# Weight prefetch ahead of blocking waits, LayerNorm statistics by chunk, and tile entry woven into the output stage

## The chip, the cores and the metric

One Trainium2 chip, all eight NeuronCores, one program that runs once per call. The metric is device time in microseconds of the slowest core. Each core has TensorE (matmuls), VectorE, ScalarE, GpSimd, and a DMA queue fed by SyncE (SP). The granted clock is the share of TensorE's full speed that the profile records; the DMA share is the mean busy share of a core's 16 DMA engines. A transfer counts as landed at the time that the trace gives for its semaphore. Most executions agree within a fraction of a per cent. In some, one die (cores 0 to 3, or 4 to 7) runs at a lower granted clock and the time is some per cent longer. Such runs are called slow here and are left out of every comparison.

## The reference, cut to what matters

One layer of a hybrid decoder over a prompt (8 sequences of 2048 tokens plus 16 meta tokens) and a sample batch (128 sequences of 8 tokens). One prompt sequence goes to each core, and 16 sample sequences.

```python
def trunk_layer(x, h0_re, h0_im, conv_buf, p):
    proj = x @ p['w_in'] + p['b_in']            # [ssm u | conv GLU pair | gate_a | gate_b], 5 x 1024 columns
    ...
    y, h_re, h_im = s5_scan(u, h0_re, h0_im, ...)          # diagonal complex SSM
    z = jax.nn.gelu(y)
    za = z * jax.nn.sigmoid(z @ p['w_glu'] + p['b_glu'])
    pa = za @ p['w_a_out']
    glu = cg[..., :CONV_WIDTH] * jax.nn.sigmoid(cg[..., CONV_WIDTH:])
    cv = causal_depthwise_conv(hist, p['conv_w'], p['conv_b'])     # width 31
    cv = jax.nn.silu(layer_norm(cv, p['conv_ln_g'], p['conv_ln_b']))
    pb = cv @ p['w_b_out'] + p['b_b_out']
    mix = (gate_a * pa + gate_b * pb) @ p['w_o'] + p['b_o']
    x = layer_norm(ALPHA * x + mix, p['ln1_g'], p['ln1_b'])        # LN1
    hdn = jnp.square(jax.nn.relu(x @ p['w_ff1'] + p['b_ff1']))     # 1024 -> 4096
    ff = hdn @ p['w_ff2'] + p['b_ff2']
    x = layer_norm(ALPHA * x + ff, p['ln2_g'], p['ln2_b'])         # LN2
    return x, h_re, h_im, new_buf
```

An entry LayerNorm precedes the layer. Outputs are both `y`, the SSM states and the last 30 conv rows.

## The kernel before

Each core first converts its weights to bf16 in a prologue (to about 461 us). It then runs four prompt tiles of 512 tokens and a sample tile of 144 columns: 128 sample tokens and the last 16 tokens of the prompt. Activations lie with the features on the partitions. A tile goes: entry (load x, LayerNorm, transpose), in-projection of `u`, SSM input, GLU in two halves, conv, gates, output projections, LN1, feed-forward, LN2, output transposes, stores.

Weights stream in units of 1 MB through three slots of `WSL`. A unit is issued where it is used, so its issue stands in SP's program order behind whatever SP waits for there (in the first tile SP waits until 522.26, and the units of the first GLU half are issued from 522.69 on, core 5):

```python
class WStream:
    def load(self, spec, first_tile):
        sl = self.nxt
        self.nxt = (self.nxt + 1) % 3
        SP.wait(self.free[sl])
        ...
        ev = self.sem[sl].add(nc.sync.dma_start(out=dst, in_=src))
        return sl, ev
    def release(self, sl, ev):
        self.free[sl] = ev
```

The SSM stage shares one 4 MB buffer, `SSMW`, between two matrices. The second, `cssc`, may land only when the SSM input matmuls are done:

```python
        ssmw_free = e_mm                       # last SSM input matmul
        SP.wait(ssmw_free)
        ev_cs = ssmw_sem.add(nc.sync.dma_start(out=SSMW[:, :], in_=dr["cssc"]))
        ...                                    # the scan, on GpSimd
        for hh in range(2):                    # the two GLU halves
            slA, evA = WS.load(("mat", "in", 0, 2 + hh), first)
            slB, evB = WS.load(("mat", "in", 0, 4 + hh), first)
            PE.wait(evA, evB)
            ...                                # 64 matmuls
```

LayerNorm sums over partitions with a matmul against a matrix of ones. It waits for all eight chunks of the residual before the first cast, and for all casts before the first statistics matmul:

```python
        def ln_stats(src_bf, sq_bf, ready_evs):
            PE.wait(ready_evs)
            bM = BK.alloc()
            for kc in range(8):
                K.MM(PS[:, bM, 0:NT], lhsT=ONESB[:], rhs=src_bf[:, kc, 0:NT], ...)
            bQ = BK.alloc()
            for kc in range(8):
                last = K.MM(PS[:, bQ, 0:NT], lhsT=ONESB[:], rhs=sq_bf[:, kc, 0:NT], ...)
        def layer_norm_r32(ready, pre_free):
            ACT.wait(ready, pre_free)
            for kc in range(8):
                ACT.raw.activation(out=SBF[:, kc, 0:NT], in_=R32[:, kc, 0:NT], func=AF.Copy)
                evs.append(ACT.mark(ACT.raw.activation(out=SQ[...], in_=R32[...], func=AF.Square)))
```

The entry of a tile (load x, `bn_stats`, normalise on VectorE, eight transposes, evacuation on ScalarE and VectorE) starts when the tile before has issued all its output transposes.

Of the kernel before, what the change touches and what calls it, by code (L numbers as in the profile page):

```python
# [13 lines left out]
NCH = 8  # L14
# [560 lines left out]
def main_loop(K, ntiles=5, stop_after=None):  # L575
# [41 lines left out]

    class WStream:
        def __init__(self):
            self.nxt = 0  # L620
            self.free = [None, None, None]
            self.sem = [DmaSem(K, f"w{i}") for i in range(3)]

        def load(self, spec, first_tile):
            sl = self.nxt
            self.nxt = (self.nxt + 1) % 3
            SP.wait(self.free[sl])
# [22 lines left out]
            return sl, ev  # L650

        def release(self, sl, ev):
            self.free[sl] = ev

    WS = WStream()

    def wmat(sl):
        return WSL[:, sl, :].rearrange("p (kc n) -> p kc n", n=512)
# [17 lines left out]
    if dbg.get("only_last"):  # L676
        tiles = [tiles[-1]]

    chk("start", 0)
    for ti, T in enumerate(tiles):  # L680
# [26 lines left out]
        if isS:  # L707
            subt = [dict(c0=0, R=128, src=[(dr["xs"][0:128, :], 0, 128)], dst=[(dr["ys"][0:128, :], 0, 128)]),
                    dict(c0=128, R=16, src=[(dr["xp"][2032:2048, :], 0, 16)], dst=[(dr["yp"][2032:2048, :], 0, 16)])]
        else:  # L710
            subt = []
            for m in range(4):
                t0 = T["tok0"] + 128 * m
                if t0 == 0:
                    src = [(dr["meta"][0:16, :], 0, 16), (dr["xp"][0:112, :], 16, 128)]
                    dst = [(dr["yp"][0:112, :], 16, 128)]
                else:
                    src = [(dr["xp"][t0 - 16:t0 + 112, :], 0, 128)]
                    dst = [(dr["yp"][t0 - 16:t0 + 112, :], 0, 128)]
                subt.append(dict(c0=128 * m, R=128, src=src, dst=dst))  # L720

        if isS:
            SP.wait(ys_free[1])
            h0_sem.add(nc.sync.dma_start(out=H0S[:, :, 0, :], in_=dr["h0re"].rearrange("p (q s) -> p q s", s=NSEQ)))
            ev_h0 = h0_sem.add(nc.sync.dma_start(out=H0S[:, :, 1, :], in_=dr["h0im"].rearrange("p (q s) -> p q s", s=NSEQ)))
            POOL.wait(state.get("g16_free"))
            scf = dr["sconv_fm"].rearrange("p (k s r) -> p k s r", k=NCH, s=NSEQ)
            for k2 in range(4):
                ev_hist = hist_sem.add(nc.gpsimd.dma_start(out=GLUS[:, 2 * k2:2 * k2 + 2, :, 0:HP],
                                                           in_=scf[:, 2 * k2:2 * k2 + 2, :, :]))  # L730
            outs.add(nc.sync.dma_start(
                out=dr["ncv_s"].rearrange("(s r) d -> s r d", r=HP)[:, 0:HP - TC, :],
                in_=dr["sconv_nat"].rearrange("(s r) d -> s r d", r=HP)[:, TC:HP, :]))

        entry_evs = []
        for st in subt:
            c0, R = st["c0"], st["R"]
            sl = state["xs_i"] % 2
            state["xs_i"] += 1
            SP.wait(xs_free[sl])  # L740
            for (src, r0, r1) in st["src"]:
                ev_ld = xs_sem[sl].add(nc.sync.dma_start(out=XS[r0:r1, sl, :], in_=src))
            chk("e1", ti)
            DVE.wait(ev_ld)
            DVE.raw.bn_stats(ST6[0:R, sl, 0:6], XS[0:R, sl, 0:512])
            e = DVE.mark(DVE.raw.bn_stats(ST6[0:R, sl, 6:12], XS[0:R, sl, 512:1024]))
            DVE.wait(e)
            e = DVE.mark(DVE.raw.bn_aggr(MV[0:R, sl, :], ST6[0:R, sl, :]))
            DVE.wait(e)
            e = DVE.mark(DVE.raw.tensor_scalar(out=RS[0:R, sl, 0:1], in0=MV[0:R, sl, 1:2], scalar1=EPS,  # L750
                                               scalar2=None, op0=ALU.add))
            chk("e2", ti)
            POOL.wait(e)
            e = POOL.mark(POOL.raw.tensor_tensor(out=RS[0:R, sl, 1:2], in0=RS[0:R, sl, 0:1], in1=NHALF[0:R, :],  # L754
                                                 op=ALU.pow))
            DVE.wait(e)
            e_n = DVE.mark(DVE.raw.tensor_scalar(out=XS[0:R, sl, :], in0=XS[0:R, sl, :], scalar1=MV[0:R, sl, 0:1],  # L757
                                                 scalar2=RS[0:R, sl, 1:2], op0=ALU.subtract, op1=ALU.mult))
            chk("e3", ti)
            PE.wait(e_n, pev["ident"])  # L760
            for half in range(2):
                b = BK.alloc()
                for k4 in range(4):
                    kc = half * 4 + k4
                    ins = K.TR(PS[:, b, k4 * 128:k4 * 128 + R], XS[0:R, sl, kc * 128:(kc + 1) * 128],
                                              IDF[0:R, 0:R])
                e_t = PE.mark(ins)
                chk("e4", ti)
                if half == 1:
                    xs_free[sl] = e_t  # L770
                eng = ACT if half == 0 else DVE
                eng.wait(e_t, pev["derv"])
                for k4 in range(4):
                    kc = half * 4 + k4
                    src = PS[:, b, k4 * 128:k4 * 128 + R]
                    if eng is ACT:
                        ACT.raw.activation(out=XB[:, kc, c0:c0 + R], in_=src, func=AF.Identity,
                                           scale=V("ln_in_g", kc), bias=V("ln_in_b", kc))
                        ins = ACT.raw.activation(out=R32[:, kc, c0:c0 + R], in_=src, func=AF.Identity,
                                                 scale=DERV[:, 0, kc:kc + 1], bias=DERV[:, 1, kc:kc + 1])  # L780
                    else:
                        DVE.raw.tensor_scalar(out=XB[:, kc, c0:c0 + R], in0=src, scalar1=V("ln_in_g", kc),  # L782
                                              scalar2=V("ln_in_b", kc), op0=ALU.mult, op1=ALU.add)
                        ins = DVE.raw.tensor_scalar(out=R32[:, kc, c0:c0 + R], in0=src,  # L784
                                                    scalar1=DERV[:, 0, kc:kc + 1], scalar2=DERV[:, 1, kc:kc + 1],
                                                    op0=ALU.mult, op1=ALU.add)
                ee = eng.mark(ins)
                BK.release(b, ee)
                entry_evs.append(ee)
# [39 lines left out]
        SP.wait(ssmw_free)  # L829
        if first:  # L830
            SP.wait(pev["winsc"])
# [388 lines left out]
        for kc in range(8):  # L1220
# [6 lines left out]
            x1_evs.append(e)  # L1227

        chk("ln1", ti)
        s2_evs = {}  # L1230
        for hh in range(2):
            hd_evs = []

# [154 lines left out]
```

## Time and profile before

| | before |
|---|---|
| five runs, us | 2947.21 to 2989.55, median 2970.75 |
| profiled run: slowest core, span | core 5, 2946.1 us |
| from in-projection to in-projection, prompt tiles, us | 542.9, 542.4, 538.7, 538.6 |
| sample tile, in-projection to end, us | 293.0 |

The tile lengths are read from TensorE's timeline: the start of the first in-projection matmul of each tile. From the page of the kernel before, the busy line and the chain that ended last (shares of the span by engine; "DMA" there is time in which the last work waited for a transfer):

```profile
PE 1726.5 (59%) x14298; PEld 976.0 (33%) x14298; DVE 682.5 (23%) x1237; ACT 704.1 (24%) x1318; POOL 578.5 (20%) x1323
PE 55%; DVE 14%; DMA 10%; ACT 9%; another core or an unknown queue 7%; issue 4%; POOL 1%; SPq 1%; DVEq 0%; ACTq 0%; POOLq 0%
```

No engine is full. The last work hangs on TensorE for 55%, and for the rest on what TensorE waits for: 10% transfers, 14% and 9% chains of VectorE and ScalarE. Those three shares are what a change of order can reach.

### The profile page before, as it was taken

The page shows a single profiled execution, that of the slowest core. Times are in us where ns is not written, and L with a number is a line of the kernel's source. Part 1 is how long each engine was busy: PE and PEld are TensorE (multiplying, and loading weights), DVE is VectorE, ACT ScalarE, POOL GpSimd, SP SyncE. Part 2 cuts the span into 40 slices and gives each one's busy share as a digit, 9 for nine tenths or more (in the row PEclk, how much of TensorE's full clock was granted, in tenths as well). Part 3 has the DMA queues.
Part 4 walks back from the last instruction along what each step waited for, and adds up shares of the span by engine and source line. Part 5 has one row for each costly group of instructions (what it writes and reads, how often), then busy time and mean ns, then how long its engine had stood idle before and what let it go on. Part 6 is the DMA issues. An engine that isn't in the chain of part 4 may idle for free.

```text
span 2946.1 us, 37746 instructions; the slowest of 8 cores (2921.0 to 2946.1 us)
## 1 busy us (share of the span) xinstructions
PE 1726.5 (59%) x14298; PEld 976.0 (33%) x14298; DVE 682.5 (23%) x1237; ACT 704.1 (24%) x1318; POOL 578.5 (20%) x1323
## 2 busy tenths in 40 slices
PE   0010004589778269795945789596468976814645
PEld 0010002336333134462423336242333633314634
DVE  4850002111221500322032021402311122131121
ACT  0000093122232211314122131322212223221322
POOL 6000000640022037001201730031065002203001
PEclk9999999797889579877976896798669787956867
DMA  9999934442223334312414431241334222595445
GB/s 113 119 137 106 114 121 132 144 138 73 86 84 103 115 128 154 101 59 65 137 56 146 152 114 57 73 129 57 143 139 144 73 86 86 106 151 177 152 150 182
DMA packets 233776, 338.81 MB, mean 115 GB/s; under 512 B 29807, under 2 KB 213295, under 8 KB 231645
## 3 DMA queue, kind: packets, MB, share of 16 engines
q1 hardware_dynamic: 209261, 299.75, 31.8%
q0 software_dynamic: 24336, 36.64, 13.4%
q8 instruction: 117, 1.92, 0.3%
q14 instruction: 62, 0.51, 0.1%
HBM read 346.37 MB, written 63.73 MB: 139 GB/s over the span
## 4 chain that ended last, share of the span: by engine, by line
PE 55%; DVE 14%; DMA 10%; ACT 9%; another core or an unknown queue 7%; issue 4%; POOL 1%; SPq 1%; DVEq 0%; ACTq 0%; POOLq 0%
PE PS L112 53%; DMA WSL<-wsc_in 5%; ACT DG L539 2%; PE PS L116 2%; DVE TMPA L1022 1%; ACT B L1201 1%; ACT B L1202 1%; DMA WSL<-wsc_ff 1%; DVE TA L327 1%; ACT B L1222 1%; DVE R L1206 1%; DVE R L1209 1%; DVE R L784 1%; DVE B L782 1%
## 5 line engine op out<-in xcount | busy, mean ns | idle before, releaser
L112 PE MATMUL PS<-B,WSL 128*128 128x512 bf16 (+1 forms) x4160 | 840.4, 368 | 365.8 <-DMA WSL<-wsc_in 153.8
L112 PEld LDWEIGHTS PS<-B,WSL 128*128 128x128 bf16 x4160 | 400.2, 103 | 802.2 <-issue 444.0
L1241 POOL TENSOR_TENSOR G<-G 128x512 bf16<-128x512 bf16 (+1 forms) x160 | 146.5, 916 | 1176.6 <-ACT G L1237 1175.2
L112 PE MATMUL PS<-G,WSL 128*128 128x512 bf16 (+2 forms) x1528 | 272.4, 337 | 30.9 <-POOL G L1241 18.4
L112 PE MATMUL PS<-GLU,WSL 128*128 128x512 bf16 (+1 forms) x1240 | 240.8, 338 | 0.8 <-DMA WSL<-dsc 0.7
L116 PE MATMUL PS<-IDF,XS 128*128 128x128 f32 (+1 forms) x144 | 34.0, 415 | 286.8 <-DVE XS L757 286.8
L112 PEld LDWEIGHTS PS<-G,WSL 128*128 128x128 bf16 x1528 | 144.1, 101 | 158.5 <-issue 42.4
L1237 ACT ACTIVATE G<-PS,VECS 128x512 bf16<-128x512 f32 (+1 forms) x160 | 100.1, 626 | 307.4 <-PE PS L112 305.1
L1253 DVE TENSOR_TENSOR R<-PS,R 128x512 f32<-128x512 f32 (+1 forms) x80 | 49.2, 615 | 502.7 <-PE PS L112 502.5
L112 PE MATMUL PS<-B,KB 128*128 128x64 bf16 (+1 forms) x1440 | 150.4, 276 | 15.0 <-DVE HB L1086 12.7
L112 PEld LDWEIGHTS PS<-GLU,WSL 128*128 128x128 bf16 x1240 | 119.2, 97 | 119.6 <-issue 1.8
L112 PEld LDWEIGHTS PS<-B,KB 128*128 128x128 bf16 x1440 | 140.4, 122 | 20.0 <-issue 17.3
L116 PEld LDWEIGHTS PS<-IDF,XS 128*128 128x128 f32 (+1 forms) x144 | 27.6, 223 | 292.7 <-issue 292.7
L116 PE MATMUL PS<-IDB,WP 128*128 128x128 bf16 x128 | 14.9, 310 | 175.9 <-ACT WT L519 130.1
L112 PE MATMUL PS<-B,ONESB 128*128 128x512 bf16 (+1 forms) x240 | 63.8, 436 | 91.1 <-ACT B L1202 85.0
L1201 ACT ACTIVATE B<-R 128x512 bf16<-128x512 f32 (+1 forms) x80 | 44.2, 553 | 274.0 <-DVE R L1188 139.4
L881 POOL TENSOR_TENSOR SCR<-SCR,XH 128x64 f32<-128x64 f32 x274 | 95.7, 349 | 39.9 <-POOL SCR L880 0.9
L1017 DVE SCALAR_TENSOR_TENSOR TMPB<-PS,TMPA 128x512 f32<-128x512 f32 (+1 forms) x15 | 9.2, 615 | 398.6 <-ACT TMPA L1015 398.6
L882 POOL TENSOR_TENSOR XH<-SCR 128x64 f32<-128x64 f32 x274 | 88.7, 324 | 40.4 <-POOL SCR L881 1.7
L879 POOL TENSOR_TENSOR SCR<-XH,ARt 128x64 f32<-128x64 f32 x253 | 87.6, 346 | 37.4 <-POOL XH L882 1.7
L519 ACT ACTIVATE WT<-PS 128x1024 bf16<-128x1024 bf16 x16 | 15.3, 1026 | 325.1 <-DMA winsc<-WT 199.3
L754 POOL TENSOR_TENSOR RS<-RS,NHALF 128x1 f32<-128x1 f32 (+1 forms) x18 | 9.9, 548 | 402.2 <-DVE RS L750 402.2
(161 smaller groups left out, 1699.7 us busy)
## 6 DMA issues: line engine op xcount, KB each, us to landing
WSL<-wsc_ff SPq DMA_DIRECT2D x80, 1024.0 KB, 5.5
WSL<-wsc_in SPq DMA_DIRECT2D x50, 1024.0 KB, 8.0
WSL<-dsc SPq DMA_DIRECT2D x40, 992.0 KB, 6.0
SSMW<-winsc SPq DMA_DIRECT2D x5, 4096.0 KB, 20.6
SSMW<-cssc SPq DMA_DIRECT2D x5, 4096.0 KB, 15.4
wsc_ff<-w_ff POOLq DMA_DIRECT2D x4, 4096.0 KB, 297.5
wsc_in<-w_in POOLq DMA_DIRECT2D x5, 2048.0 KB, 65.7
WSL<-wsc_bout SPq DMA_DIRECT2D x10, 1024.0 KB, 6.4
```

The costliest lines, as they stand in the source:

```text
L112: return self.nc.tensor.matmul(*a, **kw)
L116: return self.nc.tensor.transpose(*a, **kw)
L327: return dv(DVE.raw.tensor_tensor(out=out, in0=a, in1=b, op=op))
L539: ins = ACT.raw.activation(out=DG[:, slot, jt, :], in_=IDB[:], func=AF.Identity, scale=VECS[:, col:col + 1])
L782: DVE.raw.tensor_scalar(out=XB[:, kc, c0:c0 + R], in0=src, scalar1=V("ln_in_g", kc), scalar2=V("ln_in_b", kc), op0=ALU.mult, op1=ALU.add)
L879: POOL.raw.tensor_tensor(out=m1, in0=hprev, in1=ARt[:], op=ALU.mult)
L881: pw(POOL.raw.tensor_tensor(out=t_, in0=m1, in1=xk_view, op=ALU.add))
L882: return pw(POOL.raw.tensor_tensor(out=xk_view, in0=t_, in1=m2[:, :, ::-1], op=ALU.add))
L1201: ACT.raw.activation(out=SBF[:, kc, 0:NT], in_=R32[:, kc, 0:NT], func=AF.Copy)
L1237: e = ACT.mark(ACT.raw.activation(out=HDN[:, ol, :], in_=PS[:, b, 0:NT], func=AF.Relu, bias=V("b_ff1", oc), scale=1.0))
L1241: e2 = POOL.mark(POOL.raw.tensor_tensor(out=HDN[:, ol, :], in0=HDN[:, ol, :], in1=HDN[:, ol, :], op=ALU.mult))
L1253: e = DVE.mark(DVE.raw.tensor_tensor(out=R32[:, oc, 0:NT], in0=PS[:, b, 0:NT], in1=R32[:, oc, 0:NT], op=ALU.add))
```

## The change

Its intent is to let TensorE wait less, with the same arithmetic and the same number of matmuls. The diff, cut to its core:

```diff
 class WStream:
-    def load(self, spec, first_tile):
-        sl = self.nxt
-        self.nxt = (self.nxt + 1) % 3
-        SP.wait(self.free[sl])
+    def pump(self, upto):                       # self.specs: all units of all tiles in order of use
+        while self.issued <= min(upto, len(self.specs) - 1):
+            j = self.issued
+            if j >= 3 and (j - 3) not in self.released:
+                break
+            self._issue(j)                      # slot j % 3
+            self.issued += 1
+    def load(self, spec, first_tile):
+        idx = self.taken
+        self.taken += 1
+        self.pump(idx + 2)
+    def release(self, j, ev):
+        self.released[j] = ev
+        self.pump(self.taken + 1)
 ...
         ssmw_free = e_mm
+        WS.pump(WS.taken + 2)                   # ahead of cssc's wait
         SP.wait(ssmw_free)                      # then cssc
 ...
         def ln_stats(src_bf, sq_bf, ready_evs):
-            PE.wait(ready_evs)
             bM = BK.alloc()
-            (8 matmuls of src_bf)
             bQ = BK.alloc()
             for kc in range(8):
+                PE.wait(ready_evs[kc])
+                (matmul of src_bf[kc])
                 (matmul of sq_bf[kc])
 ...
         def layer_norm_r32(ready, pre_free):
-            ACT.wait(ready, pre_free)
+            ACT.wait(pre_free)
             for kc in range(8):
+                ACT.wait(ready[kc])
 ...
+        if ti + 1 < len(tiles):                 # after the feed-forward, ahead of LN2
+            for q in subts[ti + 1][0:2]:
+                load_x(ti + 1, q)
 ...
         for st in subt:                         # output transposes and stores of one sub-tile
             ...
+            if ti + 1 < len(tiles):
+                (entry of the next tile's sub-tile whose columns are free now)
```

Moved besides: the load of `SSMW`'s first matrix goes into the LN1 of the tile before, the conv-state copy and the history loads of the sample tile go into the last prompt tile.

## The prediction

> **What bounds the kernel now.** I read the page first, then the waits of TensorE inside one prompt tile, then the timelines of TensorE and of the DMA-issuing queue around the largest waits, last the sample tile. The program is a prologue (to about 461 us on the profiled core), four prompt tiles of 512 tokens of about 542 us each, and a sample tile of 144 columns (from 2641.8 us). The waits of TensorE in the second prompt tile (us in total, times, longest):
>
> ```profile
> PE PS L116 <- DVE XS L757: 32.1, 4, 13.0
> PE PS L112 <- DMA WSL<-wsc_in: 28.7, 2, 23.4
> PE PS L112 <- ACT R L1225: 23.8, 1, 23.8
> PE PS L116 <- ACT R L1269: 21.1, 1, 21.1
> PE PS L112 <- ACT B L1202: 19.1, 2, 9.6
> PE PS L112 <- ACT B L1040: 11.5, 1, 11.5
> ```
>
> The second, fifth and much of the first row are what the change is aimed at; rows 3, 4 and 6 are LayerNorm chains that it leaves. TensorE is busy 388 us of such a tile, so the tile is bound by TensorE plus exposed waits, one after another. The same waits stand in every prompt tile: the first DMA one is 24.5, 23.4, 21.7 and 20.2 us long.
>
> TensorE's timeline of the first tile's end (start, length, work, idle before it and releaser):
>
> ```profile
> 776.61 13.97 PE L112 MATMUL PS<-B,WSL 128*128 128x512 bf16 x64 [1.74 <-DVE B L1174]
> 800.14 5.86 PE L112 MATMUL PS<-B,ONESB 128*128 128x512 bf16 x16 [9.56 <-ACT B L1202]
> ...
> 921.67 27.79 PE L112 MATMUL PS<-G,WSL 128*128 128x512 bf16 x128 [2.11 <-POOL G L1241]
> 959.04 4.93 PE L112 MATMUL PS<-B,ONESB 128*128 128x512 bf16 x16 [9.59 <-ACT B L1202]
> 985.06 5.62 PE L116 MATMUL PS<-IDF,R 128*128 128x128 f32 x32 [21.09 <-ACT R L1269]
> 1003.67 1.94 PE L116 MATMUL PS<-IDF,XS 128*128 128x128 f32 x8 [12.98 <-DVE XS L757]
> 1011.99 1.94 PE L116 MATMUL PS<-IDF,XS 128*128 128x128 f32 x8 [6.38 <-DVE XS L757]
> ```
>
> The reader sees that the 16 statistics matmuls (ONESB) start 9.6 us after the projection, though their inputs come one chunk at a time; and that from the output transposes (985.06) to the first matmul of the next tile (1033.46) 48.4 us pass. The DMA queue's own timeline shows the head of the line:
>
> ```profile
> 522.26 0.33 SPq L867 DMA_DIRECT2D SSMW<-cssc  x1
> 522.69 41.07 SPq L649 DMA_DIRECT2D WSL<-wsc_in  x4
> ...
> 624.99 25.73 SPq L649 DMA_DIRECT2D WSL<-wsc_in  x4
> ```
>
> The 4 MB cssc load waits until the SSM input matmuls end (522.2), and the weights of the GLU stage stand behind it in program order, though one slot was free before that. They land at 546.4.
>
> [...]a wait blocks every load issued after it; the trace agrees (522.26, then 522.69). [...]a load behind cssc also pays its transfer; the 22.8 us from issue to landing of these weights, against 5.5 for feed-forward weights, agrees. [...]16 statistics matmuls take 5.86 us after an idle wait and 3.61 us directly behind the convolution. [...]dense stretches read clock 1.00 and 217 ns per 512-column matmul, and all cores average 0.83.
>
> **The change, part by part.** The arithmetic and the number of matmuls stay.
>
> (1) Weights ahead of blocking waits. A list of units is pumped up to the three slots, at loads, at releases, and once ahead of cssc. Units 2, 3, 4 of a tile (both inputs of the first GLU half and one of the second) are then there before the SSM input stage ends. Gone: 24.5+23.4+21.7+20.2 = 89.8 us; I keep 0.4 each for handover: 88. The second GLU wait, 5.1 to 5.4 us per tile, stays: unit 5 needs the slot of unit 2, free only after the first half. The cssc transfer (15.4 us median) is about as long as that half (15.3 to 16.7), so it should not lengthen this wait by more than 1 us. The winsc load, moved into the previous LN1, was hidden before (0.9 us wait ahead of SSM input): 0.
>
> (2) LayerNorm statistics per chunk. The residual chunks come every 1.75 us (13.97/8), ScalarE's two casts take 1.04 us a chunk, and ScalarE is idle there, so it keeps pace. After the projection TensorE goes straight through 16 warm matmuls, 3.5 us; the last chunk (0.8 us evacuation, 1.15 us casts) is ready at 1.95. LN1: from 790.6 to 806.0 = 15.4 now, 3.5 then, saves 11.9. LN2: 949.5 to 964.0 = 14.5, saves 11.0. The chain after it (21 to 24 us) is unchanged. Four tiles: 91.6. The convolution's LayerNorm goes from 1.5+3.6 to 3.5, 1.6 each: 6.4; gate matmuls stall after 48 on banks held until that chain ends, so they profit from its earlier end.
>
> (3) Tile boundary. Entry of a sub-tile now follows its output transposes, with x already loaded. A sub-tile's serial chain is 8.32 us now (1003.67 to 1011.99), mostly in-order VectorE: statistics to normalised 3.7, transposes 1.2 to 2, evacuations 2.6. The new order adds VectorE's 0.69 output copy to each: 9.05. First statistics 2.75 us after the first output transpose, then 3x9.05 + 8.33 + 0.2 = 38.4 against 48.4: saves 10.0, three times, 30. The overlap is thus partial: the chain of VectorE stays. At the sample tile there are two entries: 2.75 + 9.05 + 6.7 = 18.5, plus about 2 for output transposes 3 and 4 in TensorE's order, 20.5 against 46.7 (2606.4 to 2653.1): 26. This includes the 1.4 MB conv-state copy and history loads that now go earlier.
>
> (4) Inside the sample tile (2653 to 2946), TensorE is small and loads count:
>
> ```profile
> 2674.87 0.33 SPq L867 DMA_DIRECT2D SSMW<-cssc  x1
> 2675.25 26.43 SPq L649 DMA_DIRECT2D WSL<-wsc_in  x4
> ...
> 2747.70 7.24 SPq L996 DMA_DIRECT2D ncv_s<-YS  x16
> 2754.99 0.42 SPq L998 DMA_DIRECT2D ncv_p<-XS  x1
> 2755.50 9.61 SPq L649 DMA_DIRECT2D WSL<-wsc_in  x4
> ```
>
> The first GLU half starts at once, but takes 6 us, so unit 5 now queues behind cssc. At the measured 6 MB in 20.4 us (3.4 us/MB), 5 MB land about 17.5 us after SSM input, the half takes 6.9: 24.4 against 39.2, saves 15 (not 20+6). Gates: 13.6 us wait behind the 17 state stores; two units now precede them, the others don't, and banks hold until the conv LayerNorm ends (2759.6): saves 7.5. The 9.0 us wait for glu weights behind the state-output stores goes: 9. Two narrow LayerNorms, ScalarE-bound: 3.5 each, 7. The 16 feed-forward loads, three slots deep, stay. Sum 38.
>
> Total 88 + 91.6 + 6.4 + 56 + 38 = 280 us. From the profiled 2947.2 this gives 2667.
>
> **The rivals.** (A) All waits named above vanish wholly, entry included. For it: the diff interleaves boundaries and prefetches everywhere. Then 18 more at each boundary and 12 in the sample tile: about 2590 to 2610. Against: VectorE's order is unchanged, and buffers number three as before. (B) DMA takes the place of the wait: cssc delays unit 5 by several us, winsc delays feed-forward weights, or SP, blocked in a prefetch wait, delays output stores. The 20 us GLU wait is partly replaced by a longer second one: 20 to 50 us back, about 2700 to 2720. For it: DMA share is 0.92 while cssc runs. Against: a prompt tile's mean DMA share is only 0.33. (C) [...]Dense stretches already run at 1.00 and TensorE busy per prompt tile only rises from 72% to about 80%; a 5% loss on 1500 us would be 75: about 2765. (D) The loads were hidden anyway: excluded by rows that show TensorE idle.
>
> **Range and chances.** The five times run from 2947.21 to 2989.55 with median 2970.75; the profiled one is the fastest, 23.5 below the median. I add that to 2667: 2690. Low end 2650: fast executions[...]. High end 2740: rival B in full plus some of C. Faster 0.98, same 0.015, slower 0.005: to stay within 2% (59 us) four fifths of measured idle would have to come back.
>
> **What would show it.** Right: SSM input followed within 1 us by GLU matmuls in prompt tiles, with the 5 us wait between halves kept; a statistics block starting within 0.5 us of its projection at about 3.5 to 4 us; first matmul of the next tile 37 to 40 us after the first output transpose, entry transposes about 9 us apart; prompt tiles near 485 us from in-projection to in-projection, sample tile near 255 from its in-projection to the end; TensorE busy about 1710. Wrong: a new wait of TensorE on WSL over 8 us in a prompt tile (B), dense stretches under clock 0.95 in fast runs (C), or boundaries under 30 us (A).

## The result, and the profile after

The changed kernel took 2685.86 us in the median of nine runs. Eight of them were fast, 2683.44 to 2691.6 us; the ninth was slow, 2910.67. (Three more executions of it are on record beside these: 2681.65, fast, and two slow ones of 2913.63 and 2916.24.) The ratio of the fast runs is 0.908, with a 95% interval of 0.9052 to 0.9108. All outputs are right. Ratios here are the mean time of one kernel's fast runs over that of the other's of the same rounds, so they are not quite the ratio of the medians.

The busy line and the chain that ended last, from the page of the changed kernel:

```profile
PE 1722.1 (64%) x14298; PEld 981.9 (37%) x14298; DVE 681.5 (25%) x1237; ACT 710.2 (26%) x1318; POOL 578.7 (22%) x1323
PE 60%; DVE 15%; ACT 7%; another core or an unknown queue 7%; DMA 5%; issue 5%; POOL 1%; DVEq 0%; SPq 0%; ACTq 0%; POOLq 0%
```

The numbers of instructions are the same, and the busy times agree within 1%. The share of transfers on the chain fell from 10% to 5%, that of ScalarE from 9% to 7%. VectorE's did not fall.

The ledger of tiles, slowest core of each profiled run (core 5 before, core 3 after):

| | before | predicted | after |
|---|---|---|---|
| prompt tiles, us | 542.9, 542.4, 538.7, 538.6 | near 485 | 489.3, 485.0, 484.4, 469.7 |
| sample tile | 293.0 | near 255 | 265.9 |
| span | 2946.1 | 2667 | 2684.7 |

The fourth length holds the short boundary to the sample tile. These are single cores: over the eight, the sample tile takes 286.1 to 293.0 us before and 257.3 to 267.7 after. The waits of TensorE in the second prompt tile after, to be held against the first view in the prediction (us in total, times, longest):

```profile
PE PS L112 <- ACT R L1282: 23.8, 1, 23.8
PE PS L116 <- ACT R L1341: 21.1, 1, 21.1
PE PS L116 <- DVE XS L765: 20.2, 4, 5.3
...
PE PS L112 <- DMA WSL<-wsc_in: 5.5, 1, 5.5
```

The two LayerNorm chains stand as they were. The statistics row (`ACT B`, 19.1) is gone, the weight row went from 28.7 to 5.5, the entry row from 32.1 to 20.2. The timeline of the first tile shows how the weights did it (start, length, work, idle before and its releaser). First the start of the first GLU half before, then the same stages after:

```profile
546.63 16.68 PE L112 MATMUL PS<-B,WSL 128*128 128x512 bf16 x64 [24.45 <-DMA WSL<-wsc_in]
```

```profile
507.85 14.96 PE L112 MATMUL PS<-B,SSMW 32*128 32x64 bf16 x512 [0.93 <-ACT B L876]
522.74 15.74 PE L112 MATMUL PS<-B,WSL 128*128 128x512 bf16 x64
548.06 16.71 PE L112 MATMUL PS<-B,WSL 128*128 128x512 bf16 x64 [9.58 <-DMA WSL<-wsc_in]
```

The first GLU half (522.74) follows the SSM input with no wait, where 24.45 us stood before. The second half still waits, because its last unit can be issued only when the first half frees a slot: that half ends at 538.48, the unit is issued at 538.57 and lands at 547.82. The end of the same tile:

```profile
917.19 3.62 PE L112 MATMUL PS<-B,ONESB 128*128 128x512 bf16 x16
941.90 1.94 PE L116 MATMUL PS<-IDF,R 128*128 128x128 f32 x8 [21.09 <-ACT R L1341]
948.16 1.94 PE L116 MATMUL PS<-IDF,XS 128*128 128x128 f32 x8 [4.32 <-DVE XS L765]
...
979.67 5.60 PE L112 MATMUL PS<-B,WSL 128*128 128x512 bf16 x16 [2.90 <-DVE R L793]
```

LN2's 16 statistics matmuls start without idle time and take 3.62 us at a granted clock of 1.00; before they took 4.93, at 0.73, after 9.59 us of idling. ScalarE's own timeline shows why: at LN1 of the same tile its casts began when the whole projection was done, and now there is a pair for each chunk, 1.73 us apart (before, then after):

```profile
791.47 0.63 ACT L1201 ACTIVATE B<-R 128x512 bf16<-128x512 f32 x1 [31.36 <-DVE R L1188]
792.00 0.61 ACT L1202 ACTIVATE B<-R 128x512 bf16<-128x512 f32 x1
792.52 0.61 ACT L1201 ACTIVATE B<-R 128x512 bf16<-128x512 f32 x1
```

```profile
759.76 0.63 ACT L1258 ACTIVATE B<-R 128x512 bf16<-128x512 f32 x1 [19.28 <-DVE R L1242]
760.30 0.61 ACT L1259 ACTIVATE B<-R 128x512 bf16<-128x512 f32 x1
761.49 0.63 ACT L1258 ACTIVATE B<-R 128x512 bf16<-128x512 f32 x1 [0.58 <-DVE R L1242]
```

From the first output transpose (941.90) to the next in-projection (979.67) 37.8 us pass, against 48.4.

The sample tile is where the ledger falls short. Cut at events that both timelines have, it reads:

| sample tile, from to | before | after | saved |
|---|---|---|---|
| in-projection to end of SSM input | 21.7 | 28.0 | -6.3 |
| to end of second GLU half | 39.2 | 26.3 | 12.9 |
| to end of conv statistics | 33.6 | 32.4 | 1.2 |
| to end of conv output projection | 31.8 | 27.8 | 4.0 |
| to start of the SSM's gate matmuls (`glu`) | 42.6 | 35.8 | 6.8 |
| to end of `o` | 19.8 | 21.4 | -1.6 |
| LN1 | 20.2 | 15.3 | 4.9 |
| feed-forward | 60.4 | 60.0 | 0.4 |
| to the end | 23.7 | 18.9 | 4.8 |

The first row is a loss that the prediction didn't have; in it the in-projection ran 1.5 us shorter and the SSM input stage 7.8 us longer. The same 512 small matmuls, before and then after:

```profile
2665.41 1.30 PE L112 MATMUL PS<-B,SSMW 32*128 32x18 bf16 x128 [3.27 <-issue]
2670.25 1.30 PE L112 MATMUL PS<-B,SSMW 32*128 32x18 bf16 x128 [3.54 <-issue]
2673.99 0.80 PE L112 MATMUL PS<-B,SSMW 32*128 32x18 bf16 x69 [2.44 <-issue]
```

```profile
2431.50 1.31 PE L112 MATMUL PS<-B,SSMW 32*128 32x18 bf16 x128 [5.04 <-issue]
2439.90 1.31 PE L112 MATMUL PS<-B,SSMW 32*128 32x18 bf16 x128 [7.10 <-issue]
2446.12 0.70 PE L112 MATMUL PS<-B,SSMW 32*128 32x18 bf16 x58 [4.90 <-issue]
```

"issue" means that TensorE waited for nothing that the profile shows. The stops come 128 matmuls apart, which with their 128 weight loads are 256 instructions. The three stops add up to 9.2 us before and 17.0 after. What else differs in these stretches is the DMA traffic (stretch, us, busy of each engine, granted clock, DMA share, GB/s), before and then after:

```profile
2660.31:2674.79 14.48, 5.23 (x512) 4.75 (x512) 0.52 (x2) 0.47 (x2) 0.00 (x0) 0.66 0.01 3
```

```profile
2424.53:2446.82 22.29, 5.24 (x512) 4.76 (x512) 0.52 (x2) 0.47 (x2) 0.00 (x0) 0.57 0.74 167
```

The traces list a DMA queue of the kind "instruction": in each of the two stretches it moved three packets, 0.05 MB together, and on the whole page it moved 117 packets of 1.92 MB, 16 KB each. The two `--dma` views of these stretches, before and then after, have it in one row each:

```profile
q8 instruction: 3, 0.05, 1.3%
```

```profile
q8 instruction: 3, 0.05, 1.2%
```

The DMA records of the traces show what ends the stops. In the kernel before the three packets start at 2663.1, 2667.9 and 2671.4, each in or at the edge of a stop. Over all eight cores of both kernels (48 stops) TensorE goes on 1.1 to 1.8 us after the end of an instruction packet, every time. A packet takes as long after as before (median 1.09 and 1.08 us); but it starts 2.4 us after the stop begins, where it started 0.1 us after it (medians). I read the stops, therefore, as waits for the next block of 256 instructions: the 128 matmuls of a block run in 1.3 us with 18 columns, and the next packet lands 1.1 to 1.8 us before TensorE goes on. Under the traffic of the changed kernel its transfer begins later.

SP's own timeline shows where the traffic of the changed kernel comes from:

```profile
2402.21 18.11 SPq L1369 DMA_DIRECT2D yp<-YS  x4
2423.31 0.66 SPq L842 DMA_DIRECT2D YS<-h0re  x1
2424.01 3.14 SPq L843 DMA_DIRECT2D YS<-h0im  x1
2427.26 7.22 SPq L668 DMA_DIRECT2D WSL<-wsc_in  x3
```

The interleaved entry stretches the output stores over 18.1 us (8.8 before), and the loads of the sample state and of three weight units, which stand behind them on SP, start at 2423 to 2434, inside the SSM input stage (2424.5 to 2446.8). The same stops, much smaller, came in the prompt tiles: with 64 columns, the second tile's SSM input has a stop of 1.3 to 2.8 us and the fourth's one of 1.8 to 2.6 us on every core, where the kernel before has at most 1.0 us at a time.

### The profile page after: what moved, and what is told of

It is laid out like the page before. It is cut to its first block, busy times and chain, and to the rows that moved or that the text cites. A ratio compares the mean times of both kernels' runs of the same rounds, so it can differ in the third digit from the quotient of the medians.

```text
span 2684.7 us, 37695 instructions; the slowest of 8 cores (2673.1 to 2684.7 us)
## 1 busy us (share of the span) xinstructions
PE 1722.1 (64%) x14298; PEld 981.9 (37%) x14298; DVE 681.5 (25%) x1237; ACT 710.2 (26%) x1318; POOL 578.7 (22%) x1323
## 3 DMA queue, kind: packets, MB, share of 16 engines
q8 instruction: 117, 1.92, 0.3%
## 4 chain that ended last, share of the span: by engine, by line
PE 60%; DVE 15%; ACT 7%; another core or an unknown queue 7%; DMA 5%; issue 5%; POOL 1%; DVEq 0%; SPq 0%; ACTq 0%; POOLq 0%
PE PS L112 57%; ACT DG L539 3%; PE PS L116 2%; DVE TMPA L1076 2%; DMA WSL<-wsc_in 1%; DVE TA L327 1%; DMA WSL<-wsc_ff 1%; ACT B L1279 1%; DVE R L1263 1%; DVE R L1266 1%; DVE B L791 1%; ACT R L1282 1%; DVE R L793 1%; DMA CIM<-cim 1%
## 5 line engine op out<-in xcount | busy, mean ns | idle before, releaser
L112 PEld LDWEIGHTS PS<-G,WSL 128*128 128x128 bf16 x1528 | 146.6, 103 | 157.8 <-issue 42.6
L112 PE MATMUL PS<-B,KB 128*128 128x64 bf16 (+1 forms) x1440 | 150.4, 276 | 15.4 <-DVE HB L1140 12.7
L112 PEld LDWEIGHTS PS<-B,KB 128*128 128x128 bf16 x1440 | 140.5, 122 | 20.3 <-issue 17.6
L519 ACT ACTIVATE WT<-PS 128x1024 bf16<-128x1024 bf16 x16 | 15.4, 1024 | 325.8 <-DMA winsc<-WT 199.9
L116 PE MATMUL PS<-IDF,R 128*128 128x128 f32 (+1 forms) x144 | 33.5, 416 | 95.0 <-ACT R L1341 95.0
L935 POOL TENSOR_TENSOR SCR<-XH,AI2t 128x64 f32<-128x64 f32 x253 | 87.7, 347 | 0.0
## 6 DMA issues: line engine op xcount, KB each, us to landing
SSMW<-winsc SPq DMA_DIRECT2D x5, 4096.0 KB, 20.5
```

Of the source, the lines that this page charges most:

```text
L112: return self.nc.tensor.matmul(*a, **kw)
L116: return self.nc.tensor.transpose(*a, **kw)
L935: pw(POOL.raw.tensor_tensor(out=m2, in0=hprev, in1=AI2t[:], op=ALU.mult))
```

## The experiments

My theory was that the terms of the prediction stand, each by its own mechanism; that the boundary which is left is VectorE's chain; and that the sample tile loses because data traffic makes its instruction blocks late (the fetch theory; an estimate of mine from the two stretches above, at DMA shares of 0.01 and 0.74, that no run settled). The rivals: that the gain comes from one part and the others ride along, that the boundary is bound by the load of x or by the order of the stages, and that the sample tile loses to its weights. On the second GLU wait I had two readings. The first, that cssc's transfer ahead of it lengthens it, is the one that I held at the start; the second, that it is only the time a unit takes to land once its slot is free. Each call ran on one chip with the kernel before beside it: experiments 1 to 4, 5 to 8, 9 to 12. "Saved" is the mean of the fast runs of the kernel before in that call (2939.7, 2950.7 and 2950.3 us) less that of the experiment.

| experiment | fast runs, us | ratio to before [95%] | saved |
|---|---|---|---|
| e1_ln_alone | 2835.49, 2834.16 | none (two fast runs) | 105 |
| e2_ln_undone | 2789.37, 2786.26, 2789.04 | 0.9485 [0.9464, 0.9506] | 151 |
| e3_no_lookahead | 2800.29, 2795.95, 2798.5 | 0.9519 [0.9498, 0.9541] | 141 |
| e4_entry_after_stores | 2682.49, 2678.9, 2685.97 | 0.9125 [0.9102, 0.9148] | 257 |
| e5_changed_again | 2705.81, 2683.77, 2683.67, 2689.35 | 0.9119 [0.9074, 0.9164] | 260 |
| e6_cssc_late | 2718.81, 2727.15 | 0.9229 [0.9198, 0.9259] | 228 |
| e7_early_stats | 2648.02, 2643.51, 2642.0, 2639.08 | 0.8953 [0.8935, 0.897] | 308 |
| e8_four_slots | 2627.99, 2658.67, 2627.85, 2631.37 | 0.8935 [0.8873, 0.8998] | 314 |
| e9_hold_in_sample | 2688.61 | one look | |
| e10_boundary_undone | 2715.64, 2738.25, 2717.34 | 0.9244 [0.9194, 0.9295] | 227 |
| e11_cssc_after_conv | 2682.78, 2681.22, 2686.91 | 0.9095 [0.9078, 0.9111] | 267 |
| e12_combined | 2572.64, 2571.99, 2568.92 | 0.8714 [0.8698, 0.8729] | 379 |

All gave right results.

**e1_ln_alone.** The kernel before, with the statistics part of the change alone (the same lines as in the diff above).

> The kernel before with only the LayerNorm part of the change (statistics matmuls and casts wait chunk by chunk). Theory (the parts add, each is worth what its wait showed): each of eight residual LayerNorms saves 11 to 12 us, each convolution LayerNorm 1.6, sample tile 7 in all: about 105 us, ratio to before 0.965. Rival (the parts overlap or the freed time returns in later waits, so one part alone gives much less): 50 us or less, ratio above 0.98.

105 us were saved, as expected. LN1's statistics start right behind the projection and take 3.62 us. So this part needs none of the others.

**e2_ln_undone.** The changed kernel with the statistics as before.

```diff
         def ln_stats(src_bf, sq_bf, ready_evs):
+            PE.wait(ready_evs)
             (8 matmuls of src_bf, then 8 of sq_bf)
-                PE.wait(ready_evs[kc])
         def layer_norm_r32(ready, pre_free):
-            ACT.wait(pre_free)
+            ACT.wait(ready, pre_free)
-                ACT.wait(ready[kc])
```

> The changed kernel with the LayerNorm statistics as before (one wait for all chunks, all sums, then all squares). Theory that the parts add: 105 us over the changed kernel, about 2790, ratio to before 0.943. Rival (loads prefetched early are hidden behind the longer LayerNorm, so part of the loss is refunded): 80 us or less. The wait of the statistics matmuls must be back at 9.6 us in every prompt tile in both readings.

It saves 151 us, 109 less than the changed kernel in its second measurement (e5). The wait for ScalarE's casts is back in the second tile, 19.1 us in two pieces, the very numbers of the kernel before:

```profile
PE PS L112 <- ACT B L1259: 19.1, 2, 9.6
```

Taken alone or taken away, the part is worth about the same.

**e3_no_lookahead.** The list of units stays, each is issued only where it is used.

```diff
-            self.pump(idx + 2)
+            self.pump(idx)
         def release(self, j, ev):
             self.released[j] = ev
-            self.pump(self.taken + 1)
-        WS.pump(WS.taken + 2)
```

> The changed kernel with each weight unit issued only where it is used, so behind the SSM output-weight load as before; everything else of the change stays. Theory: the first GLU wait returns at 20 to 24 us per prompt tile while the second falls to 5.1 to 5.4 from the 5.5 to 9.6 of the changed kernel, net about 80 us in four prompt tiles, and 15 to 25 us in the sample tile: about 100 us, 2785, ratio 0.942. Rival (weights were hidden anyway, the 108 us of LayerNorm and the boundary made the gain): below 30 us. In the sample tile the issue waits inside the SSM input stage fall from 17 us to about 9 if the prefetched weight loads cause the rest.

119 us less saved than in e5. In the first prompt tile TensorE again waits 33.9 us for these weights, 25.0 of them in one piece:

```profile
PE PS L112 <- DMA WSL<-wsc_in: 33.9, 2, 25.0
```

The 19 us above the expectation have a cause that I had left out: no unit is loaded during the boundary any more, so the sample tile's in-projection waits 16.2 us for its first. The stops in the sample tile's SSM input shrink (11.5 us on the profiled core, 9.4 in the median of the cores, DMA share 0.01), as the fetch theory wants.

**e4_entry_after_stores.** The entry follows all output sub-tiles, x is still loaded ahead.

```diff
             ys_free[sl] = ev_o
-            if ti + 1 < len(tiles):
-                done_cols = c0 + R
-                while nxt_i < len(subts[ti + 1]) and ... <= done_cols:
-                    emit_entry_sub(ti + 1, subts[ti + 1][nxt_i], e_t)
-                    nxt_i += 1
         if ti + 1 < len(tiles):
             while nxt_i < len(subts[ti + 1]):
```

> The changed kernel with the entries of the next tile emitted after all output sub-tiles, x still loaded early. My reckoning: the four output copies end 9.3 us after the first output transpose, then 4 times 8.32 us: 42.7 us from first output transpose to first matmul of the next tile instead of 37.8, so 4.9 us at each of three boundaries and about 5 at the sample tile: 20 us in all, ratio to before 0.915. Rival (interleaving is the worth of that part, early x only a detail): 10 us or more at each boundary, 40 us or more in all.

The profiled run was slow on one die; the other die's cores are read. The boundary is 42.0 us (core 3, from 926.84), 4.2 more than in the changed kernel and as expected. Yet the total is that of the changed kernel within the noise. The difference comes back in the sample tile, which is 249.5 to 253.4 us long to its last matmul on the four clean cores, against 253.8 to 264.2 on the eight cores of the changed kernel. SP's timeline on core 0 says why:

```profile
2403.15 5.52 SPq L1369 DMA_DIRECT2D yp<-YS  x4
2411.03 0.66 SPq L842 DMA_DIRECT2D YS<-h0re  x1
```

The stores are done in 5.5 us instead of 18.1, and the state and the weights come while TensorE still does the entry. On the clean cores the DMA share in the SSM input stage is 0.30 to 0.37, and the stops are 10.3 us in the median. So weaving entry and stores together gains 4 us at each of three prompt boundaries and 3.5 at the sample tile, some 16 us, and gives about 10 of them back inside the sample tile; the few us that should be left don't stand out of the noise.

**e5_changed_again.** The changed kernel beside the next three.

> The changed kernel itself, as the reference on the same chip as the next three, since the prologue ended 6 to 7 us earlier on the chip of the first four runs. 2675 to 2690, second GLU wait 5.5 to 10 us in prompt tiles, issue waits in the SSM input stage of the sample tile about 17 us.

It repeats: 0.9119 against 0.908, intervals overlapping. Differences below some 10 us between calls are therefore taken from tile lengths, not from ratios. One of its four fast runs, the profiled one of 2705.81, is an outlier (its first tile took 507 and 505 us on cores 0 and 1), and so is 2658.67 in e8. What is "saved beyond e5" below goes by the means of the table; by medians it is 44 us for e7 and 57 for e8.

**e6_cssc_late.** If cssc delays the second GLU wait's unit, moving cssc behind the GLU must shorten that wait.

```diff
         WS.pump(WS.taken + 2)
-        SP.wait(ssmw_free)
-        ev_cs = ssmw_sem.add(... cssc)
         ...
+        if not isS:                       # behind both GLU halves; in the sample tile behind the conv
+            SP.wait(ssmw_free)
+            ev_cs = ssmw_sem.add(... cssc)
         chk("glu", ti)
```

> The changed kernel with the SSM output-weight load moved behind the GLU stage (prompt tiles) or behind the convolution (sample tile). Theory (that load delays unit 5, the last GLU weights): the second GLU wait falls to 5.1 to 5.5 us in every prompt tile (8 us less in sum) and from 13 to about 5.5 in the sample tile; 10 to 15 us faster than the changed kernel in all. Rival (unit 5 is late only because its slot comes free late[...]): waits and time unchanged within 3 us.

Missed. It was 32 us slower than e5 (means of the fast runs; the profiled run was slow on one die, so a core of the other die is read). In prompt tiles the second wait didn't shrink (5.4 to 5.8 us in most, 8.3 in the first tile of core 5), and a new one appeared: cssc now stands ahead of the conv weights, and TensorE waits 9.8 us for them in that tile:

```profile
583.31 42.91 PE L112 MATMUL PS<-GLU,WSL 128*128 128x512 bf16 x186 [9.81 <-DMA WSL<-dsc]
```

In the sample tile the second wait did fall, to 5.4 to 8.1 us from 10.3 to 14.8. Moving a 4 MB load by one stage moved the collision by one stage.

**e7_early_stats.** Statistics and normalisation of the next tile's first two sub-tiles are done on VectorE during the second feed-forward half. If the boundary is VectorE's chain, it must shorten by what is taken out of it.

```diff
         for hh in range(2):
             hd_evs = []
+            if hh == 1 and ti + 1 < len(tiles):
+                for q in subts[ti + 1][0:2]:
+                    load_x(ti + 1, q)
+                for q in subts[ti + 1][0:2]:
+                    emit_entry_stats(ti + 1, q)      # bn_stats ... normalise, split off from the entry
 ...                                       (and load_x no longer ahead of LN2)
```

> The changed kernel with mean, variance and normalisation of the next tile's first two sub-tiles done during the second half of the feed-forward. Theory (in-order VectorE chain sets the boundary): first output transpose to next tile's first matmul falls from 37.8 to about 28 us at three boundaries, from 19.5 to about 12 at the sample tile; 35 us faster in all, about 1.3%. Rival (TensorE transposes or ScalarE's evacuations and the output stores bind there): 33 us or more at a boundary, under 15 us in all.

The boundary fell from 37.8 to 27.5 us and that to the sample tile from 19.5 to 8.8, 41 us over the four; 48 us were saved beyond e5. The first boundary on core 0:

```profile
939.43 1.94 PE L116 MATMUL PS<-IDF,R 128*128 128x128 f32 x8 [21.10 <-ACT R L1352]
941.16 1.91 PE L116 MATMUL PS<-IDF,XS 128*128 128x128 f32 x8
...
966.97 13.33 PE L112 MATMUL PS<-B,WSL 128*128 128x512 bf16 x52 [2.90 <-DVE R L802]
```

The entry's first transposes (`IDF,XS`) run with no wait. x was loaded ahead in both kernels, so it is VectorE's chain, and not the load, that bound the boundary.

**e8_four_slots.** A fourth weight slot, and a lookahead of one more. If the second GLU wait is a slot that comes free too late, it must go.

```diff
-    WSL = K.sb("WSL", [128, 3, 4096], BF16)
+    WSL = K.sb("WSL", [128, 4, 4096], BF16)
-            self.pump(idx + 2)
+            self.pump(idx + 3)
-            self.pump(self.taken + 1)
+            self.pump(self.taken + 2)
 ...                                       (slot numbers modulo 4, and the other two pumps, alike)
```

> The changed kernel with four weight slots and one unit more lookahead. Theory (the second GLU wait is a slot wait, made longer by the load ahead of it): it vanishes in prompt tiles, 29 us in sum; in the sample tile the 13 us wait goes too[...], so 10 to 20 us there: 40 to 50 us faster. Rival (the DMA engines bind there): the wait moves to the convolution's weights and the gain is under 20 us.

Gone, in every prompt tile: both halves are one block. On core 0, the first tile:

```profile
525.29 29.82 PE L112 MATMUL PS<-B,WSL 128*128 128x512 bf16 x128
```

54 us were saved beyond e5: 9.8, 7.0, 10.2 and 10.1 in the prompt tiles and 20.3 in the sample tile (slowest core against core 3 of e5, the sample tile to its last matmul). The prompt tiles gain more than their waits there (9.7, 5.4, 7.0 and 6.8 us). The clock was lower with the wait, too: in the changed kernel's first tile the second half's 64 matmuls read a granted clock of 0.83 and took 16.7 us, and both halves together 32.45; here all 128 take 29.8 at 0.93. In the sample tile the wait moved on in part: TensorE waits 9.55 us for the first conv weights, which now stand behind cssc.

**e9_hold_in_sample.** Meant as the direct test of the fetch theory: no weight prefetch while the sample tile's SSM input runs.

```diff
-            self.pump(idx + 2)
+            self.pump(idx if self.hold else idx + 2)     # the same at releases; hold: in-projection and SSM input of the sample tile
```

> The changed kernel, but in the sample tile no weight unit is loaded ahead until its SSM input matmuls are done. Theory[...]: the three issue waits of the SSM input stage fall from 14 to 17 us in sum to 9 to 12 (9.2 in the kernel before), and the first GLU half then waits 5 to 9 us for its weights, so the total hardly moves. Rival (the issue waits come with the tighter order[...]): still 14 us or more.

Void. The edit moved the loads in program order, but nothing between the old place and the new one makes SP wait, so they were issued at the same time (2427.7 against 2427.3) and the stops were the same 17.1 us. Here a later line alone didn't hold a load back. A wait on a semaphore did: in the kernel before, SP waits for the SSM input matmuls, which end at 522.2, and issues cssc at 522.26.

**e10_boundary_undone.** Entry after the stores, and x loaded only then.

```diff
-        if ti + 1 < len(tiles):
-            for q in subts[ti + 1][0:2]:
-                load_x(ti + 1, q)
 ...
-            (the entry of the next tile between the output sub-tiles, as in e4)
-            (the early load of x for the third and fourth sub-tile)
```

> The changed kernel with the boundary as before: entries after all output stores, x loaded only then. From first output transpose to next tile's first matmul 48 us again at three prompt boundaries (10.5 more than the changed kernel), about 38 to 45 instead of 19.5 at the sample tile; less the 10 us that the sample tile gained in the run with the entries after the stores. About 40 to 50 us over the changed kernel, near 2730, ratio 0.926. Rival (later stages absorb it): under 25 us.

The boundary is 47.8 us, within 0.6 of the kernel before. With e4 this splits the 10 us: 5.8 from the early load of x, 4.2 from the interleaving. The boundary to the sample tile is 29.1 us and not the 38 to 45 that I expected, for most of its gain isn't undone here. In the kernel before, x stood on SP's queue behind the state loads and the conv-state copy, and was issued 22.2 us after the first output transpose (2606.38); here it stands ahead of them, 9.2 us after (2423.31). Before, then here:

```profile
2624.74 3.81 SPq L731 DMA_DIRECT2D ncv_s<-sconv_nat  x1
2628.60 0.56 SPq L742 DMA_DIRECT2D XS<-xs  x1
```

```profile
2432.52 0.42 SPq L743 DMA_DIRECT2D XS<-xs  x1
```

In all 34 us less saved than in e5, below the 40 to 50 expected for that reason and because the sample tile's SSM input got its 4 us back.

**e11_cssc_after_conv.** As e6, but cssc goes behind the conv stage, so no weight unit of GLU or conv stands behind it.

```diff
-        SP.wait(ssmw_free)
-        ev_cs = ssmw_sem.add(... cssc)
 ...
         chk("conv", ti)
+        SP.wait(ssmw_free)
+        ev_cs = ssmw_sem.add(... cssc)
```

> The changed kernel with the SSM output-weight load moved behind the convolution in all tiles, where TensorE later waits 11 us for the conv LayerNorm anyway. Theory (the load costs whatever weight load stands behind it, and here there is slack): second GLU wait 5.1 to 5.5 us, no new wait on the convolution's weights, 5 to 12 us faster than the changed kernel. Rival (there is no free place for 4 MB in the tile): again slower, as when it stood behind the GLU stage.

As fast as the changed kernel within the noise, not 5 to 12 us faster. Over 32 prompt tiles (eight cores) the second GLU wait has a median of 5.66 us, 5.77 in the changed kernel and 5.40 in the kernel before. So in prompt tiles cssc isn't the cause, and that rival is out: the wait is the time that a 1 MB unit takes to land after its slot came free (a median of 5.6 us from issue to landing for the 50 units of `wsc_in` in the changed kernel). In the sample tile cssc was part of the cause: there the second-half wait fell to 5.5 to 7.0 us, from 10.3 to 14.8. Yet the tile is hardly shorter (256.3 to 260.3 us to its last matmul over the cores, against 253.8 to 264.2).

**e12_combined.** Four slots, cssc behind the conv, statistics of the first three sub-tiles early (three x slots, paid for by placing a small staging buffer in one of them), and the sample state loaded behind the SSM input. (In program order only: as in e9, nothing makes SP wait there, and the trace has the state loads inside that stage.)

> All that helped: four weight slots, the SSM output-weight load behind the convolution, statistics and normalisation of the next tile's first three sub-tiles during the feed-forward, state loads of the sample tile behind its SSM input stage. If gains add (44 for the early statistics, 57 for the slots, some 16 for the third sub-tile, 5 to 10 for the load): 120 us under the changed kernel, 2560 to 2575. If they overlap in the sample tile: 2580 to 2600. Ratio to before 0.87 to 0.88.

2571.2 us in the mean of the fast runs, ratio 0.8714: some 4% below the changed kernel (0.8714 / 0.9119 = 0.956). The gains of e7 and e8 add up (48 + 54 beyond e5 would be 362 saved; 379 were). On core 2 of the undisturbed die the prompt tiles take 460.0, 460.4, 460.9 and 444.2 us. The largest waits left in a prompt tile are the two LayerNorm chains, 23.8 and 21.1 us.

**What the three undoings add up to.** e2, e3 and e10 cost 109, 119 and 34 us, together 261 before rounding, the whole gain. I don't read this as proof that the parts are independent: e3 pays 16 us in the sample tile that the kernel before didn't, and the conv-state copy and the history loads, which were moved, are undone in none of the three.

**The fetch theory over runs.** The sample tile's SSM input stage, medians over the eight cores (of e4, e6 and e12 over the four of the undisturbed die), from the timelines of runs that were made for other reasons:

| kernel | DMA share in the stage | stops, us | stage, us |
|---|---|---|---|
| before | 0.02 | 8.1 | 13.3 |
| e3_no_lookahead | 0.01 to 0.02 | 9.4 | 14.6 |
| e4_entry_after_stores | 0.30 to 0.37 | 10.3 | 15.5 |
| e10_boundary_undone | 0.28 to 0.36 | 10.8 | 16.1 |
| e7_early_stats | 0.53 to 0.93 | 11.4 | 16.6 |
| e6_cssc_late | 0.85 to 0.90 | 12.9 | 18.2 |
| e8_four_slots | 0.77 to 0.93 | 14.3 | 19.6 |
| changed | 0.72 to 0.89 | 15.4 | 20.6 |
| e12_combined | 0.79 to 0.88 | 16.2 | 21.6 |

The stops are long where the traffic is dense, though the order isn't strict (e3 has next to none and longer stops than the kernel before; e6 is as dense as the changed kernel). That the stops end with the landing of an instruction block is shown above. That data traffic is what makes the block late stays unproven, since e9 failed. Nor is it the weights alone: in e4 and e10 the stage holds 1.3 to 1.9 MB of weights but not the state loads, whose short packets (under 512 B) are 8272 of the changed kernel's 11347 there (slowest core), and their stops are among the short ones. No run tells the two kinds of load apart.

## Why the prediction was right, point by point

The total was right: 2690 predicted, 2685.86 measured. Two errors in it nearly cancelled. The saving was put at 280 us and is 261.4 (2946.1 less 2684.7), 18.6 too much. And 23.5 us were added because the kernel before's median lay that far above its profiled run; the changed kernel's fast runs lie within some 8 us of each other, so this add-on should have been near zero. That the total came within 5 us is luck; what holds is the four terms below, one by one.

- **Weights ahead of blocking waits (88).** The first GLU wait went wholly in all prompt tiles, 89.8 us. The second was to stay at 5.1 to 5.4 and not grow by over 1 us. It stayed; its median over all cores grew by 0.4 us, but on the profiled core it was 9.58, 5.46, 6.96 and 6.66, 7 us more than before in sum. Net about 83.
- **Statistics (91.6 + 6.4).** LN1 was to fall from 15.4 to 3.5 and is 3.45; the conv's block was to take 3.5 and takes 3.6. In sum the twelve blocks of the prompt tiles end 99.6 us sooner after the work before them. e1 and e2 put the whole part, sample tile included, at 105 and 109, where its terms sum to 91.6 + 6.4 + 7 = 105.
- **Boundary (30 + 26).** 38.4 predicted, 37.8 to 38.0 measured at the three; 20.5 predicted at the sample tile, 19.5 measured; 58 us in all. (The prediction's 9.05 for 8.32 + 0.69 should be 9.01, which changes nothing.) The entries' transposes were to come about 9 us apart and come 8.8 to 8.9 apart. e7 confirms the reason given, VectorE's chain: with part of it done earlier the boundary fell from 37.8 to 27.5 us.
- **Sample tile (38).** This is the term that was mis-sized: 27.1 measured. Of its pieces the GLU (15 predicted, 12.9), the gates (7.5; 1.2 + 4.0) and the `glu` weights (9; 6.8) fell 6.6 us short together, and the two LayerNorms (7; 4.9 and part of 4.8) were met. What the sum lacked altogether is the stretch up to the end of the SSM input, 6.3 us longer. The prediction had counted the loads that move there as free, because TensorE needed no weights from them; yet the packets of TensorE's instructions came later there (2.4 us after a stop began, against 0.1, in the median). I had the stops in front of me in the profile before (9.2 us) and passed over them as a constant.
- **Rivals.** A (all waits vanish, 2590 to 2610) is out: entry and second half wait as argued. B (the wait returns on the weights) appears only as those 7 us in prompt tiles, and no wait on weights exceeds 10 us there, though the one of 9.58 passes the 8 us that I had named as a sign of B. C (a lower granted clock in denser stretches, a possibility that no profile had shown) doesn't show in fast runs: in the changed kernel the projection before LN1 and both statistics blocks read a granted clock of 1.00, 218 ns per 512-column matmul. D (hidden loads) is out by the result.

The sum by these measurements is 83 + 100 + 58 + 27 = 268, some 6 us more than the 261.4 of the ledger. Between 2 and 3 of them went to the stops in the prompt tiles' SSM input (3.8 us on the profiled core, 1.5 before); the rest isn't attributed.

Left open: why the unit of the second half in the first tile lands 9.25 us after its issue (e11 rules cssc out there too, with waits of up to 9.0 us), and a controlled test of what delays the instruction blocks.

## What to carry to other kernels

SP's wait for the SSM input matmuls delayed the weights that stood behind it in program order (24.45 us of idle TensorE in the first tile), so issue what already has a free buffer ahead of such a wait; then count the buffers, because the wait that stays is the one that lacks a slot (a fourth slot was worth another 54 us here). VectorE's chain at the boundary gave way when part of it was done earlier, in the feed-forward: that was worth another 48 us. A wait for eight things that come one after another is worth splitting wherever the consumer can take them one at a time; that was 105 us for a few moved lines. And ask of each load that is moved earlier what else is running at its new time: in the stage of 512 short matmuls into which loads were moved here, TensorE's stops for instructions grew from 9.2 to 17.0 us, and it is not shown which of those loads, if any, did it.

## What else the traces show

- Between blocks of 256 instructions (128 matmuls and their weight loads): with 18 columns a block runs in 1.3 us, and TensorE then stops for 2.4 to 3.5 us at a DMA share of 0.01 (kernel before, core 5) and 4.9 to 7.1 us at one of 0.74 (changed kernel, core 3). With 64 columns, 512 matmuls took 14.96 us without a stop in the first prompt tile of core 3, and there were single stops of 1.3 to 2.8 us in the second and fourth. TensorE went on 1.1 to 1.8 us after the end of the block's transfer.
- Granted clock in and after small tiles: 512 back-to-back matmuls on 32-row tiles (first prompt tile, TensorE busy throughout) read a granted clock of 0.55 in the changed kernel and 0.63 in the kernel before, and took 14.96 us both times; the full-array matmuls that follow them at once in the changed kernel take 15.74 us for 64, at 0.89, against 13.97 at a clock of 1.00.
- Granted clock after a wait: the 16 statistics matmuls of 512 columns took 5.86 us at 0.61 and 4.93 us at 0.73 after waits of 9.6 us (LN1 and LN2 of the first tile, kernel before), and 3.62 us at 1.00 in the changed kernel, directly behind other matmuls, on all eight cores.
- Granted clock in dense stretches: 1.00 and 218 ns per 512-column matmul in fast runs, with all eight cores at work. The changed kernel's slow runs had the cores of one die at 0.70 to 0.78 in the mean of the run, against 0.79 to 0.86 in its fast runs.
- Loads issued from SP: in the changed kernel the median from issue to landing of a 1 MB weight unit was 5.4 to 5.6 us (9.2 us for one in the first tile, 11.1 in the sample tile's SSM input stage), that of 4 MB 15.0 us for cssc but 20.5 us for the other SSM matrix.
- The mean granted clock of a core can mislead: cores of one run of the changed kernel read 0.79 or 0.857 with spans within 12 us, and the difference lies in the prologue, in which TensorE is nearly idle (21 to 22 of 370 us busy, at a clock of 0.55 or 1.00, between 100 and 470 us).
